# Half rows of the conditioning weights, asked for in front of their first pass, in a conditioned decoder layer on one core

## The chip, the core and the metric

The kernel runs on one core of a Trainium2 chip. Time is device time of one execution in microseconds (us), lower is better. The core has five engines with a queue each: TensorE (PE; its weight loads are shown as PEld), VectorE (DVE), ScalarE (ACT), GpSimd (POOL) and SyncE (SP). SP does no arithmetic here; it issues nearly all transfers from HBM. Each queue runs strictly in its own order, and engines wait for each other through semaphores.

## The reference, cut to what matters

```
mod = (silu(c) @ w_ada + b_ada).reshape(9, D)          # D = 2048: nine vectors of 2048
h = rms_norm(x, norm_ffn1) * (1 + mod[1]) + mod[0]
x = x + 0.5 * mod[2] * swiglu(h, w_ffn1_gu, w_ffn1_down)
h = rms_norm(x, norm_mix) * (1 + mod[4]) + mod[3]
x = x + mod[5] * token_mixing(h, w_in, w_ret_branch, w_swa_branch, w_out, sinks)
h = rms_norm(x, norm_ffn2) * (1 + mod[7]) + mod[6]
x = x + 0.5 * mod[8] * swiglu(h, w_ffn2_gu, w_ffn2_down)
out = rms_norm(x, norm_final)                          # x: 256 rows of 2048
```

All in float32. `w_ada` is 2048 x 18432, 151 MB, and is used for one matrix-vector product only.

## The kernel before

**Weights of the layer.** Every matrix product runs over pieces. A raw tile (`raw`, 1 MB, four buffers) holds 512 weight columns for four blocks of 128 inputs. SP asks for it in `load` (L370). For each half of it `split` makes two parts that PE can multiply fast: ACT casts a high part (`wh`, L394), DVE subtracts it from the raw values for a low part (`wl`, L396). Both have three buffers. `products` (L379) then runs 12 matmuls for each half, called a product below; a raw tile gives two products, 24 matmuls. The activations are split in the same way: beforehand for the up products (`hh`, `hl`), piece by piece for the down products and the branch products (`a`, L429 on ACT, L430 on DVE).

**Conditioning.** The nine vectors `mod` don't run on PE. `w_ada` comes transposed, so that one row of 2048 gives one value per partition: DVE multiplies a block of 128 rows with `cact` = silu(c) in passes of 512 columns and sums (`ada_pass`, L222, four passes for each of 144 blocks). `conditioning` is a generator that yields after each pass; `tick` (called after every product) draws passes from it at `pace["rate"]` passes for each product. Before a pass, `ask` issues transfers (L285) until `pace["ahead"]` passes beyond the current one are covered. Where a row goes is told by `place`: `two_rows` gives the halves of a tile of two rows in turn (two whole rows of 2048 columns, 1 MB each, or, with `parts=4`, four half rows of 512 KB).

**Who uses that.** The first two vectors are made in another loop (`place` and `group`, L215) and aren't touched here. Three vectors run beside the last group of the first up product and then beside `ffn_up` and the first down product (`ROWS_FFN1`; half rows in that last group, then whole rows); three beside the token mixing, first into raw tiles of their own, then into `rows_x`, a free tile of two rows; one beside the second up product.

**Order.** SP's order is that of the code (`manual_schedule` for SP). The orders of DVE, ACT and PE are set by the scheduler when the kernel is built, except in the normalisations. So a transfer stands in SP's queue where the code asks for it, between the raw tiles of that place; the pass that reads it stands in DVE's queue where the scheduler puts it. A raw tile can be asked for when the `wl` of the tile four before is done.

**Banks.** PE adds into four banks `pa`, two for each product of 512 columns. A bank is free again when DVE or ACT has read it: L726 and L725 for the first feed-forward's last group, L1645 for the products of the branches.

## Time and profile before

| what | value |
|---|---|
| time, median of 3 runs | 2355.68 us (2355.55 to 2356.41) |
| time of the profiled execution | 2356.11 us |
| its span, first to last instruction | 2354.1 us |
| mean granted PE clock | 0.999 |
| HBM read | 598.60 MB, 256 GB/s over the span |
| raw tiles of 1 MB for w_ffn_gu, w_in, w_ffn_down | 144, 104, 88 transfers |
| conditioning rows of 1 MB into slot, rows_x, raw | 75, 31, 17 transfers |
| conditioning half rows of 512 KB into slot | 38 transfers |

The profiled execution lies 0.4 us above the median, and 2.0 us of it lie around the span. An engine is counted as busy while an instruction of its own runs; issuing a transfer and waiting are not counted. A row of the timeline reads: start in us, duration in us, engine, line, operation, output and inputs, count, and in brackets the idle time just before it with what ended it. The profile's chain of waits follows the work that ended last back from the end.

### The profile page before, as it was taken

Reading aid. Unit: us, or ns where it says so; the run is one execution under the profiler, and the core shown is the slowest. Engines: PE = TensorE matmul, PEld = TensorE weight load, DVE = VectorE, ACT = ScalarE, POOL = GpSimd, SP = SyncE. Lnnn points to the kernel's source line nnn. Section 1 sums busy time; section 2 is a strip of 40 time slices with the busy share of each in tenths; the row PEclk is TensorE's granted clock in tenths of the full one; section 3 lists DMA queues with packets and bytes.
Section 4 is the critical chain, followed back from the end, with each engine's and each line's share of the span. In section 5 each row is a group of like instructions: output and inputs, shape, how many; then the busy total and the mean of one; then the engine's idle time right before and its main releaser. Section 6 shows DMA issues by size and latency. Waiting matters only on the chain.

```text
span 2354.1 us, 28400 instructions
## 1 busy us (share of the span) xinstructions
PE 2333.5 (99%) x10443; PEld 1918.3 (81%) x10443; DVE 1678.3 (71%) x2610; ACT 1363.1 (58%) x1889; POOL 19.7 (1%) x28
## 2 busy tenths in 40 slices
PE   8999999999999999999999999999999999999998
PEld 5888888888888888778888888888888888888887
DVE  7789898778877768876767876676555555555656
ACT  6776665455556567774556564465455454455544
POOL 0000000000000000000000000000000000000000
PEclk9999999999999999999999999999999999999999
DMA  9989999887765899867779787754767778666553
GB/s 362 339 344 393 325 336 350 305 317 289 298 239 219 294 267 254 249 216 261 270 271 306 292 307 282 271 205 177 259 239 255 242 239 268 223 231 202 193 197 125
DMA packets 194492, 630.35 MB, mean 268 GB/s; under 512 B 113393, under 2 KB 115185, under 8 KB 128049
## 3 DMA queue, kind: packets, MB, share of 16 engines
q1 hardware_dynamic: 191858, 617.54, 75.3%
q0 software_dynamic: 1600, 9.83, 1.1%
q8 instruction: 81, 1.33, 0.2%
q10 hardware_dynamic: 896, 1.19, 0.1%
q14 instruction: 57, 0.47, 0.1%
HBM read 598.60 MB, written 4.22 MB: 256 GB/s over the span
## 4 chain that ended last, share of the span: by engine, by line
PE 97%; DVE 1%; DMA 1%; ACT 1%; issue 0%; SPq 0%; ACTq 0%; DVEq 0%
PE pa L379 95%; PE ps L1477 0%; DMA slot<-in_w_ada_dram 0%; PE pd L1393 0%; DVE slot L222 0%; DMA t<-in_b_ada_dram 0%; PE ps L379 0%; PE ps L915 0%; ACT wh L394 0%; DVE wl L396 0%; PE ps L1393 0%; PE pd L1575 0%; PE pd L1562 0%; PE pd L1576 0%; PE pd L1577 0%
## 5 line engine op out<-in xcount | busy, mean ns | idle before, releaser
L396 DVE TENSOR_TENSOR wl<-raw,wh 128x1024 fp32r<-128x1024 f32 (+1 forms) x808 | 963.7, 1202 | 496.7 <-ACT wh L394 425.2
L394 ACT CAST wh<-raw 128x1024 fp32r<-128x1024 f32 (+1 forms) x808 | 833.4, 1037 | 807.6 <-PE pa L379 785.1
L379 PE MATMUL pa<-wh,hh 128*128 128x512 f32 x2184 | 599.5, 391 | 2.5 <-ACT wh L394 0.8
L379 PE MATMUL pa<-wh,hl 128*128 128x512 f32 x2184 | 594.8, 389 | 0.0
L379 PE MATMUL pa<-wl,hh 128*128 128x512 f32 x2184 | 588.5, 389 | 0.0
L379 PEld LDWEIGHTS pa<-wh,hh 128*128 128x128 f32 x2184 | 407.6, 188 | 90.7 <-issue 2.4
L379 PEld LDWEIGHTS pa<-wh,hl 128*128 128x128 f32 x2184 | 409.9, 188 | 86.0 <-issue 0.4
L379 PEld LDWEIGHTS pa<-wl,hh 128*128 128x128 f32 x2184 | 409.6, 188 | 85.9 <-issue 0.8
L379 PE MATMUL pa<-wh,a 128*128 128x512 f32 x1824 | 452.1, 389 | 0.0
L379 PEld LDWEIGHTS pa<-wh,a 128*128 128x128 f32 x1824 | 341.6, 188 | 70.6
L222 DVE CUSTOM_DVE_ANT_0 slot<-slot,cact 128x512 f32<-128x512 f32 (+2 forms) x310 | 234.5, 805 | 22.2 <-DMA slot<-in_w_ada_dram 22.1
L379 PE MATMUL pa<-wl,a 128*128 128x512 f32 x912 | 245.1, 389 | 0.0
L379 PEld LDWEIGHTS pa<-wl,a 128*128 128x128 f32 x912 | 171.1, 188 | 35.4
L570 ACT COPY slot<-back 128x512 uint16<-128x512 uint16 x148 | 98.7, 767 | 0.0
L222 DVE CUSTOM_DVE_ANT_0 rows_x<-rows_x,cact 128x512 f32<-128x512 f32 x124 | 78.8, 688 | 25.8 <-DMA rows_x<-in_w_ada_dram 25.7
L429 ACT CAST a<-slot 128x512 fp32r<-128x512 f32 x114 | 70.7, 621 | 28.7 <-PE pa L379 28.5
L554 ACT COPY flat<-t 128x512 uint16<-128x512 uint16 x136 | 76.7, 617 | 11.7 <-DVE t L1550 8.5
L430 DVE TENSOR_TENSOR a<-slot,a 128x512 fp32r<-128x512 f32 x114 | 78.1, 686 | 0.3
L222 DVE CUSTOM_DVE_ANT_0 raw<-raw,cact 128x512 f32<-128x512 f32 (+1 forms) x72 | 48.0, 718 | 20.1 <-DMA raw<-in_w_ada_dram 20.1
L1249 ACT COPY slot<-pa 128x512 f32<-128x512 f32 x64 | 34.7, 592 | 22.6 <-PE pa L379 22.6
L379 PE MATMUL pa<-wh,home 128*128 128x512 f32 x160 | 39.5, 389 | 0.0
L222 DVE DVE_READ_ACCUMULATOR2_ANT sums<- 128x1 f32 x442 | 36.9, 84 | 0.0
(233 smaller groups left out, 1091.9 us busy)
## 6 DMA issues: line engine op xcount, KB each, us to landing
raw<-in_w_ffn_gu_dram SPq DMA_DIRECT2D x144, 1024.0 KB, 5.2
raw<-in_w_in_dram SPq DMA_DIRECT2D x104, 1024.0 KB, 6.5
raw<-in_w_ffn_down_dram SPq DMA_DIRECT2D x88, 1024.0 KB, 4.9
slot<-in_w_ada_dram SPq DMA_DIRECT2D x75, 1024.0 KB, 7.3
rows_x<-in_w_ada_dram SPq DMA_DIRECT2D x31, 1024.0 KB, 7.1
raw<-in_w_ffn_gu_dram SPq DMA_DIRECT2D x32, 768.0 KB, 6.1
slot<-in_w_ada_dram SPq DMA_DIRECT2D x38, 512.0 KB, 6.9
raw<-in_w_ada_dram SPq DMA_DIRECT2D x17, 1024.0 KB, 6.2
```

Of the source, the lines that this page charges most:

```text
L222: nc.vector.tensor_tensor_reduce(out=here, in0=here, in1=cact[:, at], scale=1.0, scalar=0.0, op0=ALU.mult, op1=ALU.add, accum_out=sums[:, ...
L379: product = nc.tensor.matmul(banks[t], act[:, j, t * P : (t + 1) * P], weights[:, j, :], start=starts and i == 0 and j == 0, stop=ends and ...
L394: cast.append(nc.scalar.copy(hi, src).ins)
L396: low.append(nc.vector.tensor_sub(lo, src, hi.bitcast(F32)).ins)
L429: nc.scalar.copy(hi, v)
L430: nc.vector.tensor_sub(lo, v, hi.bitcast(F32))
L554: nc.scalar.copy(planes[:, i, :], words(src)[:, :, i])
L570: nc.scalar.copy(into[:, :, :, i], held["turned"][:, i])
L1249: nc.scalar.copy(p, b)
```

## The change

`two_rows` always gives four half rows, the row ring stays the same from the last group on, and `pace["ahead"]` is 0 where it was `AQ` = 4: a half row is asked for in the code just in front of the first of its two passes, and no longer a row ahead. Passes, their number and their rates stay. The rows into raw tiles (`ahead` 2) stay until `rows_x` is free. Lines behind the change move up by 3 (L396 becomes L393, L285 L282, L430 L427, L726 L723) and by 5 (L1645 becomes L1640).

```diff
-    def two_rows(both=None, parts=2):
+    def two_rows(both=None):
         both = slot() if both is None else both
-        n = 2 * D // parts
-        turn = [both[:, i * n : (i + 1) * n] for i in range(parts)]
-        if parts == 2:
-            turn.reverse()
+        turn = [both[:, i * D // 2 : (i + 1) * D // 2] for i in range(4)]
...
         if final:
-            row_ring.append(two_rows(rows_home, 4))
-            set_pace(ROWS_FFN1, 192, place_row, AQ)
+            row_ring.append(two_rows(rows_home))
+            set_pace(ROWS_FFN1, 192, place_row, 0)
...
     tiles.append(slot())
-    row_ring[0] = two_rows(rows_home)
     pace["rate"] = (192 - 64) / 117
-    pace["ahead"] = AQ
     ffn_up(held, gu, tiles, EARLY, turned=range(EARLY, DFF // CH))
...
         row_ring.append(two_rows(one.tile([P, 2 * D], F32, tag="x", name="rows_x")))
-        pace["ahead"] = AQ
+        pace["ahead"] = 0
...
-    set_pace([(8, None, 0.5)], 150, two_rows(), AQ)
+    set_pace([(8, None, 0.5)], 150, two_rows(), 0)
```

What moves is seen in the order of the instructions on their engines. In these rows a number behind a name tells buffers apart; `L222 ISA slot_117,sums...` is one pass, and the row `L222 ISA sums...` behind it stores its sum.

**Place 1, the end of the first feed-forward's last group.** DVE before, from the two `wl` of the next product's first raw tile to the reads of the banks (`pa_3112`, `pa_3113`, L726):

```order
L396 TENSOR_TENSOR wl_3214<-raw_3211,wh_3213 128x1024
L396 TENSOR_TENSOR wl_3233<-raw_3211,wh_3232 128x1024
L726 TENSOR_TENSOR a_119<-pa_3112,a_119 128x512
L726 TENSOR_TENSOR a_119<-pa_3113,a_119 128x512
L725 TENSOR_TENSOR t_3185<-pa_3038,a_118 128x512
L725 TENSOR_TENSOR t_3196<-pa_3039,a_118 128x512
```

DVE with the change, the same place (L726 is L723 here):

```order
L393 TENSOR_TENSOR wl_3212<-raw_3209,wh_3211 128x1024
L393 TENSOR_TENSOR wl_3231<-raw_3209,wh_3230 128x1024
L222 ISA slot_117,sums_3227<-slot_117,cact 128x512
L222 ISA sums_3227 128x1
L222 ISA slot_117,sums_3227<-slot_117,cact 128x512
L222 ISA sums_3227 128x1
L723 TENSOR_TENSOR a_119<-pa_3110,a_119 128x512
L723 TENSOR_TENSOR a_119<-pa_3111,a_119 128x512
```

Two passes now stand between the second `wl` and the first read of a bank; before they stood ahead of the first `wl`, in a run of four.

**Place 2, the first down product.** SP before, in the middle of its first half (`raw` are weights of w_ffn_down, L285 rows of w_ada):

```order
L370 DMA raw_4536<-in_w_ffn_down_dram 128x2048
L285 DMA slot_117<-in_w_ada_dram 128x2048
L370 DMA raw_4583<-in_w_ffn_down_dram 128x2048
L370 DMA raw_4619<-in_w_ffn_down_dram 128x2048
L285 DMA slot_117<-in_w_ada_dram 128x2048
L370 DMA raw_4662<-in_w_ffn_down_dram 128x2048
```

SP with the change:

```order
L367 DMA raw_4552<-in_w_ffn_down_dram 128x2048
L282 DMA slot_117<-in_w_ada_dram 128x1024
L367 DMA raw_4599<-in_w_ffn_down_dram 128x2048
L282 DMA slot_117<-in_w_ada_dram 128x1024
L367 DMA raw_4636<-in_w_ffn_down_dram 128x2048
L282 DMA slot_117<-in_w_ada_dram 128x1024
```

A whole row behind every second raw tile has become a half row behind every raw tile. DVE before, in the same stretch; the row of the fence above that is asked for behind `raw_4536`, which waits for `wl_4392`, is the one that the passes at the end read:

```order
L396 TENSOR_TENSOR wl_4392<-raw_4369,wh_4391 128x1024
L396 TENSOR_TENSOR wl_4419<-raw_4416,wh_4418 128x1024
L430 TENSOR_TENSOR a_4410<-slot_114,a_4410 128x512
L396 TENSOR_TENSOR wl_4436<-raw_4416,wh_4435 128x1024
L396 TENSOR_TENSOR wl_4457<-raw_4454,wh_4456 128x1024
L430 TENSOR_TENSOR a_4413<-slot_114,a_4413 128x512
L222 ISA slot_117,sums_4407<-slot_117,cact 128x512
L222 ISA sums_4407 128x1
L222 ISA slot_117,sums_4407<-slot_117,cact 128x512
L222 ISA sums_4407 128x1
L396 TENSOR_TENSOR wl_4474<-raw_4454,wh_4473 128x1024
```

DVE with the change. `raw_4552` and the half row behind it wait for `wl_4406`; that half row is read by the second pair of passes here, the first pair reads the one asked for a raw tile earlier:

```order
L393 TENSOR_TENSOR wl_4406<-raw_4383,wh_4405 128x1024
L222 ISA slot_117,sums_4421<-slot_117,cact 128x512
L222 ISA sums_4421 128x1
L222 ISA slot_117,sums_4421<-slot_117,cact 128x512
L222 ISA sums_4421 128x1
L393 TENSOR_TENSOR wl_4433<-raw_4430,wh_4432 128x1024
L427 TENSOR_TENSOR a_4424<-slot_114,a_4424 128x512
L393 TENSOR_TENSOR wl_4450<-raw_4430,wh_4449 128x1024
L222 ISA slot_117,sums_4421<-slot_117,cact 128x512
L222 ISA sums_4421 128x1
L222 ISA slot_117,sums_4421<-slot_117,cact 128x512
L222 ISA sums_4421 128x1
```

Between the `wl` that lets a transfer be asked for and the pass that reads it stood three `wl` and two `a`; now two passes, two `wl` and one `a` stand there.

**Place 3, the end of the first pair of branch products.** DVE before, from the last two `wl` to the first read of a bank (L1645):

```order
L396 TENSOR_TENSOR wl_10892<-raw_10872,wh_10891 128x1024
L396 TENSOR_TENSOR wl_10934<-raw_10931,wh_10933 128x1024
L222 ISA rows_x,sums_10749<-rows_x,cact 128x512
L222 ISA sums_10749 128x1
L222 ISA rows_x,sums_10749<-rows_x,cact 128x512
L222 ISA sums_10749 128x1
L222 ISA rows_x,sums_10749<-rows_x,cact 128x512
L222 ISA sums_10749 128x1
L222 ISA rows_x,sums_10749<-rows_x,cact 128x512
L222 ISA sums_10749 128x1
L430 TENSOR_TENSOR a_11548<-slot_6389,a_11548 128x512
L1645 TENSOR_TENSOR slot_8779<-slot_8779,pa_10587 128x512
```

DVE with the change:

```order
L393 TENSOR_TENSOR wl_10939<-raw_10918,wh_10938 128x1024
L222 ISA rows_x,sums_10794<-rows_x,cact 128x512
L222 ISA sums_10794 128x1
L222 ISA rows_x,sums_10794<-rows_x,cact 128x512
L222 ISA sums_10794 128x1
L393 TENSOR_TENSOR wl_10981<-raw_10978,wh_10980 128x1024
L427 TENSOR_TENSOR a_11603<-slot_6420,a_11603 128x512
L1640 TENSOR_TENSOR slot_8810<-slot_8810,pa_10630 128x512
```

Of the four passes between the last `wl` and the read of the bank none is left there; a pair stands one `wl` further ahead.

Over the whole kernel SP issues 78 more transfers for the same bytes (31 rows and 81 rows and half rows become 62 and 128 half rows); DVE, ACT and PE have the same instructions, and PE's order differs in some places where matmuls of one product stand a little earlier or later.

## The prediction

> **What bounds the kernel now.** First the busy times of the page, then the same by stage, with stages cut where TensorE (PE) starts to run through and where it stops.

> ```profile
> span 2354.1 us, 28400 instructions
> PE 2333.5 (99%) x10443; PEld 1918.3 (81%) x10443; DVE 1678.3 (71%) x2610; ACT 1363.1 (58%) x1889; POOL 19.7 (1%) x28
> ...
> 0.00:102.10 102.10, 90.93 (x353) 66.66 (x353) 76.04 (x122) 68.48 (x117) 5.27 (x10) 1.00 0.93 352
> 102.10:374.00 271.90, 271.90 (x1203) 225.21 (x1204) 240.62 (x408) 182.93 (x259) 6.96 (x4) 1.00 0.97 351
> 374.00:377.00 3.00, 2.28 (x11) 1.60 (x10) 2.84 (x4) 1.34 (x3) 0.54 (x1) 1.00 0.72 227
> 377.00:1353.00 976.00, 976.00 (x4439) 801.61 (x4438) 739.85 (x1277) 584.22 (x858) 3.23 (x6) 1.00 0.80 274
> 1353.00:1361.00 8.00, 7.42 (x34) 5.86 (x33) 6.37 (x14) 4.31 (x5) 0.00 (x0) 1.00 0.72 294
> 1361.00:2340.20 979.20, 979.20 (x4364) 811.80 (x4364) 606.73 (x776) 519.80 (x643) 3.67 (x7) 1.00 0.67 232
> 2340.20:2354.10 13.90, 5.74 (x48) 5.53 (x47) 5.87 (x15) 2.04 (x6) 0.00 (x0) 0.80 0.31 115
> ```

> A row gives length, then busy time of PE, PEld, DVE, ACT and POOL, the granted clock, the DMA engines' busy share and GB/s. The first change in any order comes behind 200 us, so the first stage stays, and so does the last, where no pass is left. Between them PE is idle for 0.72 us around 375 and 0.58 us around 1357, and nowhere else. So this change can win at most 1.3 us (0.06%) by removing PE's waits; it can lose wherever DVE now comes late for PE. The chain of waits gives PE's pace:

> ```profile
> 102.09 261.89 PE pa L379 x1154
> ```

> That is 0.227 us a matmul: a product of 12 takes 2.72 us, a raw tile of two products 5.45, two raw tiles 10.9.

> [...]

> **Term 1: place 1, two passes ahead of a bank's read.**

> ```profile
> 373.08 1.05 ACT L394 CAST wh<-raw 128x1024 fp32r<-128x1024 f32 x1 [1.66 <-PE pa L379]
> 374.16 1.23 DVE L396 TENSOR_TENSOR wl<-raw,wh 128x1024 fp32r<-128x1024 f32 x1 [1.27 <-ACT wh L394]
> 375.30 1.28 DVE L726 TENSOR_TENSOR a<-pa,a 128x512 f32<-128x512 f32 x2
> 375.42 0.33 SPq L370 DMA_DIRECT2D raw<-in_w_ffn_gu_dram  x1
> 375.84 0.38 SPq L285 DMA_DIRECT2D slot<-in_w_ada_dram  x1
> 376.14 0.70 PE L379 MATMUL pa<-wh,hh 128*128 128x512 f32 x2 [0.72 <-ACT t L316]
> ```

> The profile puts PE's wait down to ACT's L316, since that came last. I choose L726: PE's next product needs a bank, the first L726 ends at 375.30 + 0.64 = 375.94, and PE starts 0.20 later. With the change two passes stand between that `wl` and the read. A pass takes 0.61 us (next fence), so PE starts **1.22 us** later. Nothing covers it, PE waits there already. Their half row was asked for some 10 us ahead and should be there.

> **Term 2: place 3, four passes leave a bank's read.**

> ```profile
> 1355.82 1.23 DVE L396 TENSOR_TENSOR wl<-raw,wh 128x1024 fp32r<-128x1024 f32 x1 [1.63 <-ACT wh L394]
> 1356.96 0.69 DVE L222 CUSTOM_DVE_ANT_0 rows_x<-rows_x,cact 128x512 f32<-128x512 f32 x1
> 1357.57 0.69 DVE L222 CUSTOM_DVE_ANT_0 rows_x<-rows_x,cact 128x512 f32<-128x512 f32 x1
> ...
> 1359.41 0.69 DVE L430 TENSOR_TENSOR a<-slot,a 128x512 fp32r<-128x512 f32 x1
> 1360.01 1.28 DVE L1645 TENSOR_TENSOR slot<-slot,pa 128x512 f32<-128x512 f32 x2
> 1360.84 0.70 PE L379 MATMUL pa<-wh,hh 128*128 128x512 f32 x2 [0.58 <-DVE slot L1645]
> ...
> 1349.88 0.42 SPq L285 DMA_DIRECT2D rows_x<-in_w_ada_dram  x1
> ```

> Starts follow each other by 0.61 for a pass, 1.14 for a `wl` (1355.82 to 1356.96), 0.60 for an `a` (1359.41 to 1360.01). With the change the half row is asked for where the row was, at 1349.88. With 5.9 us to landing (below) its passes end at 1357.0, the `wl` at 1358.2, the `a` at 1358.8, the first read at 1359.4, and PE, which stopped at 1360.26, goes on without a stop: **-0.58 us**.

> **Term 3: half rows that are late.** The landing of a half row behind a raw tile isn't in the trace, so bounds from the nearest rows (minimum, median, maximum in us, each line behind the tile it is of, and the half rows of the last group):

> ```profile
> L285 SPq DMA_DIRECT2D slot<-in_w_ada_dram x28: 383/424/1429, 384.7 to 653.9; - x28
> ...
> DMA to landing us min/median/max: 6.9/7.4/10.3
> ...
> L285 SPq DMA_DIRECT2D rows_x<-in_w_ada_dram x24: 383/424/862, 1210.1 to 1476.2; - x24
> ...
> DMA to landing us min/median/max: 6.8/7.1/10.2
> ...
> L370 SPq DMA_DIRECT2D raw<-in_w_ffn_gu_dram x76: 327/328/340, 1647.8 to 2055.6; - x76
> ...
> DMA to landing us min/median/max: 4.7/4.9/7.8
> ...
> slot<-in_w_ada_dram SPq DMA_DIRECT2D x34, 512.0 KB, 6.7
> ```

> Below it is bounded by a raw tile that is mostly alone (4.7), above by a whole row behind a raw tile (7.1 to 7.4). The whole row's second MB costs 7.1 + 0.42 - 4.9 = 2.6 us over the raw tile (0.42 from one issue to the next, 375.42 to 375.84), half of it 1.3: a half row lands in 5.8 to 6.1, I take **5.9**. Speaking for more: the same transfer took 6.7 in the last group, but there the DMA engines were at 0.97, and in the stages that matter they are at 0.80.

> [...]

> Now the loop of place 2. From the `wl` that frees a raw tile (end 375.39 above) to the half row's issue 0.45, landing L, two passes 1.22, `wl` 1.14, `a` 0.60, `wl` 1.14, and that second `wl` frees the raw tile two further on: 4.55 + L. PE needs 10.9 for two raw tiles. With 5.9 the loop is 10.45 and DVE catches up by 0.4 in each turn; **above L = 6.35 DVE falls behind in each turn.** Before, the row was asked for once in those 10.9 us, with 0.45 + 7.4 + 1.22 + 1.14 = 10.2 in its loop, so the pace was much the same; what goes is the reserve. In PE's order five products (13.6 us) lie between the one that lets `wl_4406` be made and the one that needs `wl_4472`, behind the passes. They have to hold 2.31 (cast and `wl`, 373.08 to 375.39), 0.45, L, 1.22, 1.14 and 0.20 to PE: 5.3 + L, so 2.4 us are left at 5.9. Before, six and two thirds (18.2 us) lay between `wl_4392` and the need for `wl_4474`, and with L = 7.4 there were 5.5 us left. How late rows come now:

> ```profile
> DVE rows_x L222 <- DMA rows_x<-in_w_ada_dram: 25.7, 18, 2.6
> DVE slot L222 <- DMA slot<-in_w_ada_dram: 22.1, 18, 3.3
> ```

> In 36 waits the longest are 2.6 and 3.3 us, in the old reserve. These counts grow (the passes stand one raw tile behind the issue, not two), and DVE's idle share of 29% holds them. Only the longest reach past 2.4: three of them by 0.4 us make **+1.2 us**, my value. From below it is 0, from above the drift with L = 7.1.

> Costed at nothing: 78 more issues on SP at 0.42 us, 33 us, beside SP's waits for `wl` (a late SP would delay raw tiles, 0.42 us against the 2.4 above); the same passes on DVE; the second up product, where one half row comes in some five products.

> **Sum.** 1.22 - 0.58 + 1.2 = +1.8 us on the span of 2354.1 (execution 2356.11, median 2355.68): **2357.5 us** for a median.

> **Rivals.**
> - *The loop falls behind (slower).* If half rows land in 6.8 rather than 5.9 (above: 6.7 in a loaded stage), each turn loses 0.45. The paced stretch of the first down product is 117 - 48 = 69 products, 188 us, 17 turns: 7.7 + 0.9 - 2.4 = 6.2 us. The branch products from 1250 to 1480 are 21 turns of the same rows, 9.5, less some 2.5 since the rate of 0.95 leaves out one half row in twenty, so 9.5 - 2.5 + 0.9 - 2.4 = 5.5 us. With 0.6 from terms 1 and 2: +12.3, 2368. At 7.1 it is +24, below 6.35 nothing. For it: the maximum of 10.3, and the smaller reserve. Against it: the DMA share of 0.80, bytes unchanged and spread more evenly. 27%.
> - *The profile's releaser is right in place 1.* If PE waited for ACT's L316, the passes cost nothing there and the 0.72 us stays: with -0.58 alone 2355.1. Against it: the 0.20 from L726 to PE, as from L1645 in place 3 (1360.65 to 1360.84). 12%.
> - *The later request isn't later in fact.* SP runs as far ahead as four raw tiles let it, so a half row comes early enough anyway, no pass is late for PE, and term 3 is 0: 2356.3. 12%.

> **How the numbers follow.** Forecast 46%, rivals 27, 12 and 12%, 3% for a gain from what the rows don't show. About 0.2% (4.7 us) is what a measurement of this kernel can tell from no change. The second and third rival and the forecast lie within it: 70%. Slower by more: 27%, the first rival. Faster by more: 3%. The range goes down to the most that can be won (2355.7 - 1.3 = 2354.4), and up to the first rival's 2368, which leaves out its upper half (some 13%) and the 3%.

> **What would show it.** Term 1: PE idle before the matmul behind L723 near 375 grows from 0.72 to about 1.9. Term 2: no idle near 1357. Term 3: half rows into `slot` and `rows_x` at 5.8 to 6.1 median; DVE's waits for them up from 48 us to over 100, and PE still busy between 490 and 660 and from 1210 to 1480. PE rows there that wait for `wl` again and again, with half rows over 6.35, would show the first rival. The prediction is wrong if PE's matmuls take other than 0.227 us or if waits appear in stages that have no half rows.

## The result, and the profile after

| | before | with the change |
|---|---|---|
| median of 6 runs each | 2356.07 us (2355.55 to 2357.60) | 2375.63 us (2371.38 to 2380.53) |
| profiled execution, its span | 2356.11, 2354.1 us | 2379.08, 2377.3 us |

The ratio is 1.0081 with an interval of 1.0071 to 1.0092: **slower by 0.8%**, and outside the range of the prediction. The profiled execution lies 3.5 us above the median. First the busy times of the page, then the stages, with columns as before (length, then PE, PEld, DVE, ACT, POOL with their counts, granted clock, DMA share, GB/s):

```profile
span 2377.3 us, 28471 instructions
PE 2343.8 (99%) x10443; PEld 1919.0 (81%) x10443; DVE 1678.9 (71%) x2610; ACT 1363.1 (57%) x1889; POOL 18.7 (1%) x28
...
102.10:374.00 271.90, 271.90 (x1205) 225.15 (x1204) 237.45 (x399) 182.13 (x258) 5.75 (x4) 1.00 0.97 344
374.00:390.00 16.00, 14.06 (x60) 11.22 (x59) 13.76 (x25) 10.48 (x16) 2.17 (x4) 0.89 0.86 325
390.00:480.00 90.00, 90.00 (x399) 74.53 (x398) 64.13 (x112) 43.52 (x50) 0.00 (x0) 1.00 0.87 307
480.00:720.00 240.00, 231.27 (x997) 186.70 (x996) 177.87 (x298) 119.65 (x144) 0.00 (x0) 0.99 0.80 274
720.00:1200.00 480.00, 479.53 (x2243) 389.96 (x2242) 359.60 (x627) 311.38 (x523) 1.61 (x3) 1.00 0.78 252
1200.00:1400.00 200.00, 195.39 (x856) 159.60 (x855) 146.26 (x251) 114.44 (x150) 0.00 (x0) 1.00 0.80 273
1400.00:2330.00 930.00, 930.00 (x4125) 769.89 (x4124) 571.89 (x730) 495.72 (x609) 3.67 (x7) 1.00 0.71 238
```

The busy share of PE is still 99%, so the share tells nothing; the count of matmuls in a stretch does. The same stretches before:

```profile
374.00:390.00 16.00, 15.28 (x72) 12.35 (x71) 14.54 (x26) 11.00 (x17) 2.16 (x4) 1.00 0.82 274
...
480.00:720.00 240.00, 240.00 (x1061) 198.78 (x1060) 189.78 (x303) 132.66 (x159) 0.00 (x0) 1.00 0.78 290
...
1200.00:1400.00 200.00, 199.42 (x881) 164.84 (x880) 151.15 (x249) 117.44 (x145) 0.00 (x0) 1.00 0.85 300
```

At 0.227 us a matmul, place 1 lost 12 (2.7 us), the first down product 64 (14.5 us) and the branch products 25 (5.7 us): 22.9 of the 23.2 us by which the span grew (four more were lost between 720 and 1200, and two gained ahead of 374). The second up product, which has half rows too, lost none. What the wait view has of DVE's waits for conditioning rows (total, times, longest); before, the totals were 22.1 us for `slot` and 25.7 us for `rows_x`:

```profile
DVE slot L222 <- DMA slot<-in_w_ada_dram: 108.0, 83, 2.9
DVE rows_x L222 <- DMA rows_x<-in_w_ada_dram: 81.0, 52, 3.5
```

The chain of waits in the first down product shows a loop, here two of its turns (start, length, what):

```profile
602.92 0.33 SPq L367
...
603.29 8.03 DMA slot<-in_w_ada_dram
...
612.04 0.60 DVE slot L222
612.65 1.14 DVE wl L393
613.79 0.60 DVE a L427
614.39 1.15 DVE wl L393
...
615.93 8.18 DMA slot<-in_w_ada_dram
...
627.19 1.15 DVE wl L393
...
628.78 7.91 DMA slot<-in_w_ada_dram
```

A `wl` lets SP ask for a raw tile and, right behind it, a half row; the half row takes 8 us; DVE stands at its pass and makes the two `wl` behind it late; the second of them lets SP ask again. The first turn took 12.6 us (603.29 to 615.93), the second 12.9. That is near the prediction's 4.55 + L, with landings L of 8.0 and 8.2, and PE needs the two raw tiles every 10.9 us. The landings of all half rows there, and of those in the second up product (minimum, median, maximum in us, each behind the line it belongs to):

```profile
L282 SPq DMA_DIRECT2D slot<-in_w_ada_dram x39: 328/432/1603, 483.2 to 688.3; - x39
...
DMA to landing us min/median/max: 5.6/7.5/8.9
...
L282 SPq DMA_DIRECT2D slot<-in_w_ada_dram x30: 419/426/436, 1687.4 to 2052.1; - x30
...
DMA to landing us min/median/max: 5.7/6.0/7.9
```

Where one half row comes in some five products they land as forecast; in the first down product, where one comes behind every raw tile, in 7.5. Beside the branch products, where nearly every raw tile has one behind it, the half rows of which the profile tells the landing (44 between 1200 and 1500) landed in a median of 6.3 us and a mean of 6.7.

### The profile page after: what moved, and what is told of

Read it like the earlier page. It is cut to its first block, busy times and chain, and to the rows that moved or that the text cites. A ratio compares the mean times of both kernels' runs of the same rounds, so it can differ in the third digit from the quotient of the medians.

```text
span 2377.3 us, 28471 instructions
## 1 busy us (share of the span) xinstructions
PE 2343.8 (99%) x10443; PEld 1919.0 (81%) x10443; DVE 1678.9 (71%) x2610; ACT 1363.1 (57%) x1889; POOL 18.7 (1%) x28
## 3 DMA queue, kind: packets, MB, share of 16 engines
q8 instruction: 81, 1.33, 0.2%
## 4 chain that ended last, share of the span: by engine, by line
PE 86%; DMA 7%; DVE 5%; issue 1%; ACT 0%; SPq 0%; DVEq 0%; ACTq 0%
PE pa L376 83%; DMA slot<-in_w_ada_dram 4%; DVE wl L393 2%; DMA rows_x<-in_w_ada_dram 2%; DVE slot L222 1%; DVE a L427 1%; PE ps L1472 0%; PE pd L1388 0%; DMA x_sb<-in_x_dram 0%; DMA raw<-in_w_ada_dram 0%; SPq L367 0%; DVE rows_x L222 0%; PE ps L376 0%; PE pa L1117 0%; DVE raw L222 0%
## 5 line engine op out<-in xcount | busy, mean ns | idle before, releaser
L393 DVE TENSOR_TENSOR wl<-raw,wh 128x1024 fp32r<-128x1024 f32 (+1 forms) x808 | 965.4, 1204 | 389.2 <-ACT wh L391 334.4
L222 DVE CUSTOM_DVE_ANT_0 slot<-slot,cact 128x512 f32<-128x512 f32 (+2 forms) x310 | 237.1, 802 | 108.3 <-DMA slot<-in_w_ada_dram 108.0
L222 DVE CUSTOM_DVE_ANT_0 rows_x<-rows_x,cact 128x512 f32<-128x512 f32 x124 | 80.9, 689 | 81.0 <-DMA rows_x<-in_w_ada_dram 81.0
L427 DVE TENSOR_TENSOR a<-slot,a 128x512 fp32r<-128x512 f32 x114 | 78.0, 685 | 0.2 <-ACT a L426 0.2
L222 DVE CUSTOM_DVE_ANT_0 raw<-raw,cact 128x512 f32<-128x512 f32 (+1 forms) x72 | 48.0, 718 | 14.8 <-DMA raw<-in_w_ada_dram 14.8
L222 DVE DVE_READ_ACCUMULATOR2_ANT sums<- 128x1 f32 x442 | 36.5, 83 | 0.0
## 6 DMA issues: line engine op xcount, KB each, us to landing
slot<-in_w_ada_dram SPq DMA_DIRECT2D x132, 512.0 KB, 6.3
rows_x<-in_w_ada_dram SPq DMA_DIRECT2D x62, 512.0 KB, 6.2
```

The lines of the kernel that those rows point to most:

```text
L222: nc.vector.tensor_tensor_reduce(out=here, in0=here, in1=cact[:, at], scale=1.0, scalar=0.0, op0=ALU.mult, op1=ALU.add, accum_out=sums[:, ...
L393: low.append(nc.vector.tensor_sub(lo, src, hi.bitcast(F32)).ins)
L427: nc.vector.tensor_sub(lo, v, hi.bitcast(F32))
```

## The experiments

Theory **A**: half rows shorten the lead. The *lead* of a row is the number of `wl` in DVE's queue between the `wl` that lets the row be asked for and the first pass that reads it. It is fixed when the kernel is built, and was counted in the orders over 60 `wl` of the first down product (the 180th to the 240th of the program):

| kernel | lead of the rows there |
|---|---|
| before | 3 (13 rows), 4 (4 rows) |
| with the change | 2 (29 half rows), 3 (4) |
| half rows, asked for four passes ahead | 2 (29), 3 (4) |
| whole rows, asked for in front of their pass | 3 (12), 4 (5) |
| half rows, passes held | 2 and 3, 3 and 4, or 4 and 5 |

So the lead follows from the size of a row and not from the setting of the passes ahead. That the scheduler puts a pass where, by its own reckoning, the row has landed would explain this; its reckoning was not looked at, so this is an inference. Rivals: **B**, what costs is that rows are asked for late (`ahead` 0); **C**, what costs is twice as many transfers of half the size.

**Half rows alone**

```diff
-            set_pace(ROWS_FFN1, 192, place_row, 0)
+            set_pace(ROWS_FFN1, 192, place_row, AQ)
...
-        pace["ahead"] = 0
+        pace["ahead"] = AQ
...
-    set_pace([(8, None, 0.5)], 150, two_rows(), 0)
+    set_pace([(8, None, 0.5)], 150, two_rows(), AQ)
```

> Half rows as in the changed kernel, but asked for four passes ahead as before. Theory A (the size of the rows sets the lead: with half rows the scheduler puts each pair of passes two low weight tiles behind its request, whatever the setting of passes ahead, so the loop of landing 6.9 to 7.2 us plus 4.55 us overruns the 10.9 us of two raw tiles): as slow as the changed kernel, 2371 to 2380, PE idle about 8 to 9 us in the first down product. Rival B (the later request is what costs): near the kernel before, 2356 to 2359. Rival C (twice as many, smaller transfers cost by themselves): as the changed kernel, as A.

2371.79 us (2368.58 to 2374.36), ratio to before 1.0067 (1.0054 to 1.0079). This speaks against B. PE had 6.0 us of idle time between 480 and 720 (8 to 9 were expected) and lost nothing at place 1: in the built order a pair of passes stands ahead of the last `wl` there, and none between it and the read of the bank.

**The late request alone.** The kernel before, with `AQ` turned into 0 at its four places:

```diff
-            set_pace(ROWS_FFN1, 192, place_row, AQ)
+            set_pace(ROWS_FFN1, 192, place_row, 0)
...
-    pace["ahead"] = AQ
+    pace["ahead"] = 0
...
-        pace["ahead"] = AQ
+        pace["ahead"] = 0
...
-    set_pace([(8, None, 0.5)], 150, two_rows(), AQ)
+    set_pace([(8, None, 0.5)], 150, two_rows(), 0)
```

> Whole rows as before, each asked for in front of its first pass (passes ahead 0 at the three places the change sets to 0, and in the last group). Theory A: the scheduler keeps three to four low weight tiles between a request and its passes, so the kernel is as before, 2355 to 2358. Rival B (late request): as the changed kernel, 2368 to 2380. Rival C: as before.

2356.83 us (2355.38 to 2361.95), ratio 1.0007 (0.9998 to 1.0016): no difference that can be told, so B falls. The two halves make 15.7 and 0.7 us, together 3 less than the change; of these three kernels only the change puts two passes in front of the bank's read at place 1.

**The lead alone.** The changed kernel with its half rows, requests and counts; only a pass may not start before an older `wl`, the one that stands five, four or three before the newest in the code. The number in the line was -6, -5 or -4:

```diff
         low.append(nc.vector.tensor_sub(lo, src, hi.bitcast(F32)).ins)
         del low[:-1]
+        lows.append(low[-1])
+        del lows[:-12]
...
-                        ada_pass(k, w, sums, q, first=first)
+                        with tc.issue_after(lows[-5]):
+                            ada_pass(k, w, sums, q, first=first)
```

> The hold again, one low weight tile less than the run with three to four: of the two passes of a half row the first may stand two low weight tiles behind the request as in the changed kernel, the second three. Theory A: the first down product's loop holds one pass instead of two and one low weight tile less, 0.45 + L + 0.61 + 1.14 = 2.2 + L (with an a tile 2.8 + L), against 10.9 us; with landings of 7.0 to 7.2 it has 0.9 us in hand and only the longest landings (over 8.1) reach PE: 2357 to 2364, between the changed kernel and the run with one more. If the lead doesn't matter: 2371 to 2380.

> The changed kernel with the same half rows, the same requests in the same places on the queue, and the same number of transfers; only each pass may not start before an older low weight tile is made, which puts passes three to four low weight tiles behind their request instead of two. Theory A (the short lead is what costs): the idle time of the first down product and of the branch products goes; what stays is place 1 near 375 (1.2 us of wait and some 1.7 us of half clock behind it), so 2357 to 2360. Rivals B and C (late request as such, or the transfers as such): no better than the changed kernel, 2371 to 2380.

> As the run before, with one more low weight tile of lead (passes four to five behind their request). Theory A: as good or better, since at place 1 only one pass is left in front of the bank's read: PE waits 0.72 + 0.61 = 1.33 us there, under the pause that was followed by a half clock, 2356 to 2358. Rivals B and C: 2371 to 2380.

| lead | time, us | ratio to before |
|---|---|---|
| 2 (the change) | 2375.63 (2371.38 to 2380.53) | 1.0081 (1.0071 to 1.0092) |
| 2 and 3 | 2363.20 (2361.46 to 2364.18) | 1.0028 (1.0017 to 1.0039) |
| 3 and 4 | 2358.39 (2356.88 to 2359.03) | 1.0009 (1.0000 to 1.0018) |
| 4 and 5 | 2356.27 (2355.94 to 2356.45) | 1.0001 (0.9992 to 1.0010) |

All three came in as A said; C falls. The rows of the run with a lead of 3 and 4, DVE's waits first, then its landings in the first down product and its stages:

```profile
DVE slot L222 <- DMA slot<-in_w_ada_dram: 12.8, 15, 3.7
DVE rows_x L222 <- DMA rows_x<-in_w_ada_dram: 9.3, 7, 2.8
...
L282 SPq DMA_DIRECT2D slot<-in_w_ada_dram x39: 328/432/1408, 480.6 to 671.1; - x39
...
DMA to landing us min/median/max: 5.6/7.4/8.7
...
480.00:720.00 240.00, 240.00 (x1061) 198.72 (x1060) 193.60 (x313) 132.29 (x159) 0.00 (x0) 1.00 0.84 295
...
1200.00:1400.00 200.00, 200.00 (x884) 165.64 (x883) 153.62 (x254) 118.29 (x146) 0.00 (x0) 1.00 0.87 295
```

The half rows land as late as in the changed kernel (7.4 against 7.5 us), and PE runs through: it is not the landing that costs, but the passes that stand too near to their request. With a lead of 3 and more the 0.58 us of place 3 goes too (884 matmuls against 881).

**Where it costs.** `two_rows` gets its argument `parts` back, with 4 as what it takes by itself, and `ahead` stays 0. Half rows only up to the end of the first down product:

```diff
-        row_ring.append(two_rows(one.tile([P, 2 * D], F32, tag="x", name="rows_x")))
+        row_ring.append(two_rows(one.tile([P, 2 * D], F32, tag="x", name="rows_x"), 2))
...
-    set_pace([(8, None, 0.5)], 150, two_rows(), 0)
+    set_pace([(8, None, 0.5)], 150, two_rows(None, 2), 0)
```

> Half rows only in the last group, the second part of the first up product and the first down product; whole rows again beside the branch products and the second up product (all requests in front of their passes). Theory A: the loss of place 1 (1.2 us of wait, with a half clock behind it 2.9) and of the first down product (8.7 us of idle time and what slow restarts add), 11 to 16 us in all: 2367 to 2372; PE runs through from 1200 to 1480 but for 0.58 us. If the loss comes from the number of transfers over the whole program it is shared by their number (62 of the 78 more half rows' worth stand elsewhere or here in like parts), some half: 2363 to 2368.

2370.43 us (2366.96 to 2375.84), ratio 1.0062 (1.0050 to 1.0075). In its profiled execution the loop sets in already at the end of the first up product (PE idle for 2.96 us at 475, behind a pass that had waited 4.3 us for its half row): 24 matmuls are lost between 390 and 480 and 30 between 480 and 720. And half rows only beside the branch products (and in the last group, as before):

```diff
+    row_ring[0] = two_rows(rows_home, 2)
     pace["rate"] = (192 - 64) / 117
...
-    set_pace([(8, None, 0.5)], 150, two_rows(), 0)
+    set_pace([(8, None, 0.5)], 150, two_rows(None, 2), 0)
```

> The other part alone: whole rows in the second part of the first up product, the first down product and the second up product, half rows beside the branch products. Theory A: the idle time of the branch products (4.6 us less the 0.58 of before) and what restarts add, no loss before 720: 2360 to 2364. With the run before it the two losses add to that of the changed kernel, some 20 us.

2360.89 us (2355.78 to 2364.61), ratio 1.0021 (1.0012 to 1.0030). The two are 14.4 and 4.8 us over before, together 19.2 against the change's 19.6: within their intervals the losses add, and neither kernel has half rows in the second up product. The second kernel's times scatter most, and one of its eleven executions, 2355.78 us, shows no loss.

**Another queue.** The requests of the half rows of both feed-forwards and of the branch products go to GpSimd's queue, so that none stands behind a raw tile's request:

```diff
-            nc.sync.dma_start(
+            (nc.gpsimd if pace["pool"] else nc.sync).dma_start(
```

> The changed kernel with one link of the loop cut in another place: the half rows of the last group, the first up and down product and the branch products are asked for on GpSimd's queue instead of SyncE's, so that a request waits only for the last passes over its half of the slot and no longer stands behind a raw tile's request that waits for a low weight tile. It comes some six low weight tiles ahead of its passes. Theory A: DVE's waits for half rows fall from 189 us to under 60, PE's idle time in the first down product and the branch products goes: 2355 to 2360, by what happens at place 1. If half rows cost by how they share the DMA engines with raw tiles, the queue makes no difference: 2371 to 2380. A cost of GpSimd's own requests, which no run shows yet, would show as waits for half rows that grew.

2371.99 us (2370.62 to 2379.19), ratio 1.0074 (1.0056 to 1.0093): the time is a miss. DVE's waits fell as expected and PE had no idle time between 480 and 720. It waited elsewhere (9.8 us between 1200 and 1400, 1.5 between 390 and 480, 2.8 behind 1400). First the waits of DVE and PE, then the raw tiles between 1220 and 1300 (the last line is the landing of all twelve).

```profile
DVE rows_x L222 <- DMA rows_x<-in_w_ada_dram: 15.1, 9, 4.8
DVE slot L222 <- DMA slot<-in_w_ada_dram: 13.2, 12, 2.8
...
PE pa L376 <- ACT wh L391: 12.3, 8, 3.4
...
L367 SPq DMA_DIRECT2D raw<-in_w_in_dram x6: 328/436/3630, 1221.5 to 1263.4; - x6
L367 SPq DMA_DIRECT2D raw<-in_w_swa_branch_dram x6: 328/726/1278, 1267.2 to 1293.4; - x6
...
DMA to landing us min/median/max: 8.1/16.9/19.7
```

Half rows that wait only for their place are asked for early: 35 of the 62 into `rows_x` were issued by 1200 us, against 9 in the changed kernel. Raw tiles then land in up to 19.7 us (4.8 to 7.2 in the changed kernel in the same stretch), and ACT's cast comes late for PE. It looks as if the place behind a raw tile in SP's queue, which makes the loop, also kept half rows from crowding out raw tiles. That is argued, not shown: the transposes of `back`, which stand in SP's queue between the raw tiles, took up to 14.0 us to issue there (up to 4.2 in the changed kernel), and in the first down product, with half rows on the same queue of GpSimd, raw tiles landed in a median of 5.5 us.

**A version with the lead of before or more, where it matters.** The hold of 4 and 5 from the first down product on, but not for the rows in raw tiles (near 909 that hold had cost 0.74 us); the last group asks four passes ahead without a hold:

```diff
+    def held_back():
+        if pace["hold"]:
+            return tc.issue_after(lows[-pace["hold"] - 1])
+        return nullcontext()
...
-            set_pace(ROWS_FFN1, 192, place_row, 0)
+            set_pace(ROWS_FFN1, 192, place_row, AQ)
...
+    pace["ahead"], pace["hold"] = 0, 3
     down_product(Whole(tiles), dn, gate, KF, spare_of(held), *calls)
...
+    pace["hold"] = 0
     set_pace([(7, 2, None), (6, None, None), (5, None, 1.0)], 192 / 0.95, place_row, 2)
...
-        pace["ahead"] = 0
+        pace["ahead"], pace["hold"] = 0, 3
```

> Half rows as in the changed kernel with passes held four to five low weight tiles behind their request, but only where half rows and loose places meet: from the first down product on, beside the branch products behind their head, and in the second up product; the last group asks four passes ahead with no hold, as before. By theory A this keeps the 0.72 us at place 1 as before, loses nothing in the down and branch products, and has neither the 0.58 us of place 3 nor the 0.74 us near 909 that the hold put on the rows in raw tiles: idle time in the middle 0.72 us against 1.30 of before, 2355.0 to 2356.0, 0.6 us under the kernel before at best, which is less than can be told from no change.

2354.66 us (2354.25 to 2355.53), 0.3 us under the expected range, against 2356.07 (2355.43 to 2357.85) of before: 1.4 us less, ratio 0.9994 (0.9986 to 1.0003), so at most a small gain, which the interval doesn't tell from none. Its one idle time of PE in the middle is 0.72 us at place 1, which explains 0.6 of the 1.4. Another 0.6 of the difference between the two profiled executions lies in the first stage, ahead of anything that the change moves: the 353rd matmul starts at 101.45 us here and at 102.09 before. So not all of the 1.4 us is won by the rows.

## Why the prediction was wrong, step by step

**What bounds the kernel: right.** PE ran through, and no more than 1.3 us could be won; the best version found is 1.4 us lower, which can't be told from no change.

**Term 1 (two passes ahead of the read at place 1, +1.22): right in the wait, and short by what came behind it.** PE's rows there, in the changed kernel:

```profile
376.58 0.70 PE L376 MATMUL pa<-wh,hh 128*128 128x512 f32 x2 [1.94 <-DVE a L723]
377.12 0.63 PE L376 MATMUL pa<-wh,hl 128*128 128x512 f32 x2
377.59 0.88 PE L376 MATMUL pa<-wl,hh 128*128 128x512 f32 x2
378.26 1.05 PE L376 MATMUL pa<-wh,hh 128*128 128x512 f32 x2
379.12 1.05 PE L376 MATMUL pa<-wh,hl 128*128 128x512 f32 x2
379.97 1.05 PE L376 MATMUL pa<-wl,hh 128*128 128x512 f32 x2
380.82 0.80 PE L376 MATMUL pa<-wh,hh 128*128 128x512 f32 x2
381.46 0.62 PE L376 MATMUL pa<-wh,hl 128*128 128x512 f32 x2
```

The wait is 1.94 = 0.72 + 1.22, put down to L723, so the rival by which the profile's releaser was right falls. Behind it some eight matmuls follow each other by 0.427 us instead of 0.227 (378.26 to 379.12 for two): 1.6 us which the sum didn't have. The granted clock is 0.51 from 377.70 to 381.20 (last section).

**Term 2 (the four passes that leave place 3, -0.58): wrong in this kernel.** The passes left, but the loop comes late there:

```profile
1383.96 0.70 PE L376 MATMUL pa<-wh,hh 128*128 128x512 f32 x2 [1.51 <-DVE slot L1640]
```

The step assumed a half row that lands in 5.9 us and no lag carried in. With the lead of before, the 0.58 us did go (the runs with the hold).

**Term 3 (half rows that are late, +1.2): the mechanism right, one size wrong, and that decided.** The loop, its 4.55 us, the threshold of 6.35 and the reserve of 2.4 us were the prediction's own, and the turn of 12.6 us at a landing of 8.0 confirms the first two. The step that failed is the size of the landing, "a half row lands in 5.8 to 6.1, I take 5.9": it measured a median of 7.5 and a mean of 7.1 over the first down product, and a mean of 6.7 beside the branch products, both above the threshold of 6.35. The value came from a raw tile of a quiet stage (4.9) and the lower values of a skewed set (7.1 of whole rows with 7.4 and up to 10.3 beside it). A loop whose turns follow each other adds up the *mean* of what it waits for, late ones included. The first rival's own formula with the measured mean gives 17 turns x (4.55 + 7.1 - 10.9) + 1.2 - 2.4 = 11.6 us for the down product (with the median of 7.5 it would be 18.8). 14.5 were lost: 8.7 us of idle time in 12 stops, some 0.3 us more at each restart (an estimate: what is left of the 14.5, over the 12), and 1.6 us of a second stretch at half the clock behind a 2.07 us pause that ends at 640.51 (granted clock 0.50 from 640.60 to 644.00). Why the same transfer lands 1.5 us later there is only partly seen: the landing falls with the time since the request of the half row before (correlation -0.51 over 36 half rows, but -0.26 with a lead of 3 and 4), and that half row was still on its way in 29 of the 36 cases. That the load alone makes it was not tried.

**The first rival (the loop falls behind, 27%) is what happened.** Its time of 2368 was at L = 6.8, and the range had left out just its upper half. That its 24 us at 7.1 come near the 19.6 measured is in part luck: 12 of them are for the branch products, where 5.7 were lost and the formula gives 21 x 0.35 - 2.5 + 0.8 - 2.4 = 3.3 with the mean of 6.7, and none of the 24 is for the half clock. **The third rival (the later request is no later in fact)** is half right: by itself the setting `ahead` changed nothing (2356.83 us), but the half rows shortened the lead by another way, in the order that the scheduler built.

Of what was costed at nothing, the 78 more issues on SP stayed so: the runs with the hold have them and lose nothing by them.

## What to carry to other kernels

Before a transfer is split or moved, count in the built order how much work stands between what lets it be asked for and what reads it, and set that time against the mean landing in that very stage, not against the median of a quiet one. Here the scheduler gave the smaller transfer the shorter lead; a hold on the consumer restores it without touching the transfers. The place of a request behind others in a queue was here, as it looks, also a throttle: with it gone, 35 half rows instead of 9 were asked for by 1200 us, and between 1220 and 1300 us raw tiles landed in up to 19.7 us instead of 7.2.

## What the runs showed of the hardware that was not expected

**The granted clock of PE halved for 3.4 us behind some pauses of 2 us.** The run with a lead of 3 and 4 was profiled three times; each has the same pause of 1.95 us at place 1. Its eleven times had fallen in two groups.

> The hold with three to four low weight tiles once more, for the clock behind place 1: its eleven times fall in two groups, 2356.9 to 2357.3 (four, the profiled one among them, in which the matmuls behind the 1.95 us pause kept 0.227 us) and 2358.0 to 2359.0 (seven). If the upper group is executions in which some eight matmuls behind the pause run at half the clock, as in the changed kernel, a profile of 2358 us or more shows them at 0.427 us behind 377, and one under 2357.5 doesn't. If the groups have another cause, a profile of the upper group shows 0.227 us throughout.

> A second look at the same, with the same expectation: 2358 us or more with some eight matmuls at 0.427 us behind 377, or under 2357.5 without.

The first took 2357.46 us, the second 2358.55. Their windows behind the pause, the first execution's, then the second's:

```profile
377.00:380.80 3.80, 3.73 (x16) 3.11 (x17) 3.80 (x7) 1.75 (x3) 0.00 (x0) 1.00 1.01 416
...
377.00:380.80 3.80, 3.80 (x11) 3.00 (x10) 3.80 (x8) 1.74 (x3) 0.00 (x0) 0.56 0.84 339
```

The granted clock is 1.00 in one and 0.56 in the other, with 16 matmuls against 11: the two groups are executions without and with it. In these profiles it didn't go by the pause's length alone. Pauses of 1.94 to 1.95 us were followed by it in three of six (changed kernel, lead of 2 and 3, one of the three with 3 and 4), those of 2.07 us (changed kernel) and 2.96 us (half rows up to the first down product) both. Those of 1.33 us (lead of 4 and 5), 1.46 (requests on GpSimd's queue), 1.51 and 1.54 (changed kernel) weren't, and neither were those of 3.12 and 3.43 us with the requests on GpSimd's queue, with 1.00 granted in the 8 us behind each. The stretches around two pauses of the changed kernel:

```profile
374.00:377.70 3.70, 1.76 (x9) 1.17 (x8) 3.70 (x9) 1.25 (x3) 0.54 (x1) 1.00 1.04 425
377.70:381.20 3.50, 3.50 (x10) 2.72 (x9) 3.50 (x8) 1.71 (x3) 0.37 (x1) 0.51 0.74 302
638.00:640.60 2.60, 0.53 (x3) 0.14 (x3) 2.60 (x6) 1.15 (x2) 0.00 (x0) 1.00 0.98 406
640.60:644.00 3.40, 3.40 (x9) 2.63 (x10) 3.40 (x6) 1.27 (x4) 0.00 (x0) 0.50 0.40 108
```

**Landings of one and the same transfer differed by half.** Of 36 half rows in the first down product of the changed kernel 15 landed in 5.6 to 6.5 us and 21 in 7.0 to 8.9, none between. The two heaps are not sharp in other runs: with a lead of 3 and 4 five of 36 lie between, with 4 and 5 eight. What makes the late ones is open.
